# Splitting a weight row in one operation of 1024 columns instead of two of 512

## The chip, the cores and the metric

The kernel runs on one core of one Trainium2 chip. The metric is the device time of one execution in microseconds. Before the change the median of three runs is 2045.59 us (2045.24 to 2045.6).

## What is computed

A decoder trunk of two layers over 256 tokens with a model width of 2048, all in fp32. Cut to what matters here:

```python
# layer 0
u = rms_norm(x) @ w_in[0]
pooled = causal_multiscale_pool(u[..., :1536])            # 4 groups, windows 2/4/8/16
token_out = einsum(pooled, pool_w) * pool_scale
mem_out = memory_cross_attention(u[..., 1536:], mem, w_mem_kv[0])
x = x + concat([token_out, mem_out]) @ w_out[0]
x = x + squared_relu(rms_norm(x) @ w_ff1[0]) @ w_ff2[0]   # 2048 -> 8192 -> 2048
# shared keys and values, then layer 1
k1, k2, v = split(rms_norm(x) @ w_kv)
u = rms_norm(x) @ w_in[1]
token_out = rms_norm(differential_attention(q1, q2, k1, k2, v))
mem_out = memory_cross_attention(u[..., 1536:], mem, w_mem_kv[1])
x = x + concat([token_out, mem_out]) @ w_out[1]
x = x + squared_relu(rms_norm(x) @ w_ff1[1]) @ w_ff2[1]
```

## The kernel before

**Weights as rows and quads.** All weights lie in HBM in the order of use, in rows of 128 partitions by 1024 columns. A row holds eight blocks of 128 columns, or two **quads** of four blocks (512 columns). SP loads a row with one DMA (L139) into one of four `raw` buffers (RAWS, L27), up to three rows ahead of the row that is being prepared (LOADS).

**The split.** TensorE multiplies in fp32r, a rounded fp32, and the kernel keeps precision by splitting each weight in two: `Feed._split` (L152) lets ScalarE (ACT) copy the weight into `hi_ring` rounded (L157), and VectorE (DVE) subtract that from the weight and put the remainder into `lo_ring` (L158). Both rings have six slots of 512 columns (SLOTS); `Feed._slots` (L143) gives out one slot or two adjacent ones, goes back to slot 0 where two don't fit, and says no while one of them is in use. The activations are split in the same way (L369, L300).

**The order of the work.** The program runs twice. The first run, on a stand-in, only lists what is needed: every quad is a job `("N", number)` in `Plan.jobs`. `Plan.close` (L70) makes of it `prep`, the order in which the weights are split, and `loads`, the order of the rows. In the second run `Feed.quad` (L208) calls `Feed.fill` (L196) as each quad begins, and `fill` prepares everything up to three jobs ahead (AHEAD) through `Feed._prepare` (L162). `Feed.used` (L226) gives a quad's slot back when its four blocks have been multiplied. Small work of other parts (scores, transposes, sums) is queued with `at` and issued by `tick` after each quad, between the matmuls. The engines' instruction orders are settled when the kernel is compiled, by the dependences between the tiles.

**Who reads a quad.** `a_part` (L377) takes two blocks at a time: two matmuls of the rounded parts with 512 columns of split activations (L391), then two of the remainders with 256 (L393). `wide_step` (L412) reads a whole quad as the moving side, for two halves of the tokens, three matmuls each: rounded, rounded, remainder (L417, L418, L419). `c_tile` (L400) takes one block with three matmuls of 256 columns (L405 to L407), and `group_w` (L1013) does the same for the pooling maps.

**Stages in time.** From the start: memory keys and values of layer 0 (`wide_step`, 32 quads, with the loads and splits of the memory and of x beside them), memory queries, the pooling mixer (`u`, `pw`) with the memory attention between, the output projection (`out_tiles`, L1028, `wo`), the feed-forward block (`ffn`, L648). Then the shared keys and values, memory keys and values of layer 1, the queries with the differential attention between them, memory queries, output projection, feed-forward block.

`out_tiles` begins with three output tiles side by side, one in each of three PSUM banks, from those inputs that are there first; when the last inputs are there, the three are finished one after the other and the fourth tile takes the bank of the first, once `resid_add` (L637) has added both its halves to the residual (L638, L639). GpSimd (POOL) squares and sums the residual beside it (L624, L625) for the next norm, which PE reads as `st_x` (L430).

**The feed-forward block** multiplies half of its second weight by a scheme of seven products for eight. For these its rows go to `slab` buffers, and jobs `("S", slab, part)` split them, some with 1024 columns at once, in the same rings. Three of its output tiles carry one slab's jobs, so a slab job is never more than a few quads away there. Jobs `K` and `L` are sums that DVE makes for a slab.

Of the kernel before, what the change touches and what calls it, by code (L numbers as in the profile page):

```python
# [55 lines left out]
class Plan:  # L56
# [13 lines left out]
    def close(self):  # L70
        prep = []
        for job in self.jobs:

            late = job[0] == "S" and job[1] % 32 > 28
            if job[0] == "S" and job[2] == 0 and not late:
                prep.insert(max(0, len(prep) - KOFF), ("K", job[1]))
            if late and job[2] == 1:
                prep.append(("L", job[1]))
            prep.append(job)
        self.prep = prep  # L80
        self.where = {job: i for i, job in enumerate(prep)}
        self.loads = []
        self.need = {}
        for p in prep:
            if p[0] == "K":
                self.loads += [("S", p[1], 0), ("S", p[1], 1)]
            elif p[0] == "L":
                self.loads.append(("S", p[1], 1))
            elif p[0] == "S" and p[2] == 0 and ("S", p[1], 0) not in self.loads:
                self.loads.append(("S", p[1], 0))  # L90
            elif p[0] == "N" and p[1] % 2 == 0:
                self.loads.append(("N", p[1] // 2))
            self.need[p] = len(self.loads) - 1
        rows = sorted(self.loads, key=lambda r: r[0] == "N" and 8 * r[1] + 8 > self.npos)
        self.row = {r: h for h, r in enumerate(rows)}
        of = {}
        pos = 0
        for what in self.entries:
            of.setdefault(pos // 8, []).append(what)
            pos += what[4]  # L100
        self.order = []
        for r in rows:
            self.order += of[r[1]] if r[0] == "N" else self.slabs[r[1]][r[2]]


class Feed:
# [55 lines left out]
    def _prepare(self, p):  # L162
        sub, add = self.nc.vector.tensor_sub, self.nc.vector.tensor_add
        self.load(self.plan.need[p] + 1 + LOADS)
        if p[0] == "N":
            r = ("N", p[1] // 2)
            c = p[1] % 2 * 512
            if not self._split(p, self.raw[r][:, c : c + 512], 1):
                return False
            if c:  # L170
                del self.raw[r]
            return True
        ra, rb = self.raw[("S", p[1], 0)], self.raw.get(("S", p[1], 1))
        t1 = self.t1[1 if p[1] % 32 > 28 else p[1] % 2]

        def both():
            t2 = rb[:, 0:512].unsqueeze(1).to_broadcast([P, 2, 512])
            two = ra.rearrange("p (a c) -> p a c", a=2)
            sub(two, t2, two)

        if p[0] in "KL":
            add(t1, ra[:, 0:512], rb[:, 0:512])
            sub(rb[:, 0:512], t1, rb[:, 512:1024])
            if p[0] == "L":
                both()
            return True
        src, n = ((ra, 2), (t1, 1), (rb, 2), (ra, 2))[p[2]]
        if not self._split(p, src, n):
            return False
        if p[2] == 0 and ("K", p[1]) in self.plan.need:  # L190
            both()
        if p[2] == 3:
            del self.raw[("S", p[1], 0)], self.raw[("S", p[1], 1)]
        return True
# [1182 lines left out]
```

## Time and profile before

| | |
|---|---|
| median of 3 runs | 2045.59 us |
| the profiled execution | 2044.93 us |
| its span, first to last instruction | 2043.1 us |
| PE busy, matmuls | 2037.2 us, 11060 |
| DVE busy | 1716.2 us, 3215 instructions |
| ACT busy | 1349.8 us, 2505 instructions |
| POOL busy | 51.9 us, 67 instructions |
| DMA | 390.75 MB, 191 GB/s on average |
| casts of `raw` on ACT (L157) | 1193 of 512 columns, 620 ns each |
| remainders of `raw` on DVE (L158) | 1193 of 512 columns, 695 ns each |
| granted TensorE clock | 1.0 of full speed |

PE is TensorE's matmuls, and their ends are modelled, so a busy PE may still hide short waits. In the lists of groups a line has the source line, the engine, the operation, the tile that is written and the tiles that are read, the shape and the count; behind the first bar the busy time in us and the mean of one in ns, behind the second the idle time of the engine just before, and what ended most of it. In the timeline a line begins with the start in us from the span's begin and the length in us, and ends with the idle time before it in square brackets, if there was any. A remainder's span on DVE or a cast's on ACT overlaps that of the next operation a little, so that operations queued without a gap start closer together than their lengths.

### The profile page before, as it was taken

To read this page: it belongs to the slowest core of one execution; us is meant where nothing else is said; L and a number is where in the kernel's file an instruction comes from. 1 tells how busy PE (TensorE), PEld (TensorE's weight loads), DVE (VectorE), ACT (ScalarE), POOL (GpSimd) and SP (SyncE) were. 2 spreads that over 40 slices of the span, in tenths; PEclk is the share of its full clock that TensorE was granted. 3 is DMA by queue.
4 is the path that set the end of the run, shared out by engine and by line. 5 is a ranking of instruction groups with operands and counts; after the bars stand their busy time and mean duration, and the time that the engine had idled before them with its cause. 6 is when DMAs were issued, how large, how long until landed. Compare 5 with 4: busy or idle time off the path is not lost.

```text
span 2043.1 us, 32257 instructions
## 1 busy us (share of the span) xinstructions
PE 2037.2 (100%) x11060; PEld 1755.3 (86%) x11060; DVE 1716.2 (84%) x3215; ACT 1349.8 (66%) x2505; POOL 51.9 (3%) x67
## 2 busy tenths in 40 slices
PE   9999999999999999999999999999999999999999
PEld 8888888888888888888888888888888888888888
DVE  8888889889879978999766687889879978988997
ACT  7765566666666756768665697566657666666764
POOL 0001200000000000000000000310000000000000
PEclk9999999999999999999999999999999999999999
DMA  9556556555555555655565543656555555565564
GB/s 314 178 181 190 188 174 206 197 196 197 186 201 202 189 207 191 207 169 182 194 228 186 170 140 103 196 166 207 196 196 205 186 196 196 186 210 195 196 209 135
DMA packets 110470, 390.75 MB, mean 191 GB/s; under 512 B 12256, under 2 KB 14944, under 8 KB 110304
## 3 DMA queue, kind: packets, MB, share of 16 engines
q1 hardware_dynamic: 110160, 388.59, 57.1%
q8 instruction: 86, 1.41, 0.3%
q14 instruction: 80, 0.66, 0.1%
q10 hardware_dynamic: 144, 0.10, 0.0%
HBM read 386.54 MB, written 2.10 MB: 190 GB/s over the span
## 4 chain that ended last, share of the span: by engine, by line
PE 99%; ACT 1%; DVE 1%; issue 0%
PE x_bank L391 33%; PE x_bank L393 16%; PE wo L391 6%; PE p L746 5%; PE p L747 5%; PE p L748 5%; PE wo L393 3%; PE u L391 2%; PE ff L391 2%; PE u L393 1%; PE k L417 1%; PE k L419 1%; PE v L417 1%; PE k L418 1%; PE v L419 1%; PE v L418 1%
## 5 line engine op out<-in xcount | busy, mean ns | idle before, releaser
L157 ACT CAST hi_ring<-raw 128x512 fp32r<-128x512 f32 x1193 | 736.7, 620 | 529.5 <-PE x_bank L391 308.0
L158 DVE TENSOR_TENSOR lo_ring<-raw,hi_ring 128x512 fp32r<-128x512 f32 x1193 | 817.2, 695 | 206.7 <-ACT hi_ring L157 165.5
L391 PE MATMUL x_bank<-fx,hi_ring 128*128 128x512 f32 x1920 | 602.1, 395 | 0.0
L393 PEld LDWEIGHTS x_bank<-fx,lo_ring 128*128 128x128 f32 x1920 | 361.0, 188 | 83.6
L393 PE MATMUL x_bank<-fx,lo_ring 128*128 128x256 f32 x1920 | 377.4, 278 | 0.0
L391 PEld LDWEIGHTS x_bank<-fx,hi_ring 128*128 128x128 f32 x1920 | 301.4, 189 | 9.3
L391 PE MATMUL x_bank<-z,hi_ring 128*128 128x512 f32 x960 | 301.1, 395 | 0.0
L158 DVE TENSOR_TENSOR lo_ring<-slab,hi_ring 128x1024 fp32r<-128x1024 f32 x188 | 230.1, 1224 | 54.3 <-ACT hi_ring L157 53.6
L157 ACT CAST hi_ring<-slab 128x1024 fp32r<-128x1024 f32 x188 | 196.9, 1047 | 73.1 <-PE x_bank L391 36.2
L393 PEld LDWEIGHTS x_bank<-z,lo_ring 128*128 128x128 f32 x960 | 180.5, 188 | 41.7
L393 PE MATMUL x_bank<-z,lo_ring 128*128 128x256 f32 x960 | 188.8, 278 | 0.0
L391 PE MATMUL wo<-cat,hi_ring 128*128 128x512 f32 x512 | 162.5, 398 | 0.5 <-DVE resid L639 0.5
L391 PEld LDWEIGHTS x_bank<-z,hi_ring 128*128 128x128 f32 x960 | 151.9, 189 | 6.5 <-ACT room L672 0.4
L393 PEld LDWEIGHTS wo<-cat,lo_ring 128*128 128x128 f32 x512 | 95.9, 188 | 21.7
L672 ACT COPY room<-x_bank 128x512 f32<-128x512 f32 x180 | 104.9, 583 | 2.0 <-PE x_bank L393 2.0
L393 PE MATMUL wo<-cat,lo_ring 128*128 128x256 f32 x512 | 101.4, 279 | 0.0
L746 PE MATMUL p<-hi_ring,sit 128*128 128x512 f32 x256 | 100.5, 393 | 0.0
L747 PE MATMUL p<-hi_ring,sit 128*128 128x512 f32 x256 | 100.2, 391 | 0.0
L748 PE MATMUL p<-lo_ring,sit 128*128 128x512 f32 x256 | 99.7, 389 | 0.0
L391 PEld LDWEIGHTS wo<-cat,hi_ring 128*128 128x128 f32 x512 | 79.1, 189 | 2.2 <-PE wo L393 0.9
L717 ACT ACTIVATE room<-room 128x256 f32<-128x256 f32 x128 | 53.2, 416 | 39.1 <-DVE room L300 39.1
L746 PE MATMUL p<-hi_ring,z 128*128 128x512 f32 x192 | 75.2, 392 | 0.0
(313 smaller groups left out, 3102.3 us busy)
## 6 DMA issues: line engine op xcount, KB each, us to landing
raw<-in_w SPq DMA_DIRECT2D x595, 512.0 KB, 4.0
slab<-in_w SPq DMA_DIRECT2D x124, 512.0 KB, 3.3
resid<-in_x SPq DMA_DIRECT2D x8, 256.0 KB, 5.9
room<-in_w SPq DMA_DIRECT2D x4, 512.0 KB, 4.2
memraw<-in_mem SPq DMA_DIRECT2D x4, 512.0 KB, 3.6
out_y<-resid SPq DMA_DIRECT2D x16, 128.0 KB, 1.8
memraw<-in_mem SPq DMA_DIRECT2D x7, 256.0 KB, 6.3
raw<-in_w SPq DMA_DIRECT2D x3, 256.0 KB, 3.5
```

Of the source, the lines that this page charges most:

```text
L157: self.nc.scalar.copy(hi, src)
L158: self.nc.vector.tensor_sub(lo, src, hi.bitcast(F32))
L391: nc.tensor.matmul(ps, hi, xs[:, k, :], start=first and c == 0, stop=False)
L393: nc.tensor.matmul(ps[:, T : 2 * T], lo, xs[:, k, 0:T], start=False, stop=last and c == len(ks) - 1,)
L417: nc.tensor.matmul(ps[t], xl, hi, start=k == 0, stop=False)
L418: nc.tensor.matmul(ps[t], xh, hi, start=False, stop=False)
L419: nc.tensor.matmul(ps[t], xh, lo, start=False, stop=k == NK - 1)
L672: nc.scalar.copy(x, ps)
L717: at(3, lambda: nc.scalar.activation(stage[i % 8], y[:, 0:T], AF.Square))
L746: nc.tensor.matmul(ps, a[1], hi, start=first, stop=False)
L747: nc.tensor.matmul(ps, a[0], hi, start=False, stop=False)
L748: nc.tensor.matmul(ps, a[0], lo, start=False, stop=last)
```

## The change

`Plan.close` makes a set `wide` of the rows whose two quads are split in one operation. A row is in it if it isn't one of the first two, if it is whole, and if no job other than a quad's stands within eight places of its first quad in the order of preparation. That leaves out nearly all of the feed-forward blocks, whose slab jobs are always near. `_prepare` then splits a wide row with its first quad: one cast and one subtraction of 1024 columns, into two adjacent slots. The two halves are handed to the two quads, each with its own slot to give back, and the second quad's preparation has nothing left to do.

```diff
@@ -91,6 +91,14 @@
             elif p[0] == "N" and p[1] % 2 == 0:
                 self.loads.append(("N", p[1] // 2))
             self.need[p] = len(self.loads) - 1
+
+        other = [i for i, p in enumerate(prep) if p[0] != "N"]
+        self.wide = {
+            p[1] // 2
+            for i, p in enumerate(prep)
+            if p[0] == "N" and p[1] % 2 == 0 and p[1] >= 4 and 4 * p[1] + 8 <= self.npos
+            and all(abs(i - o) > 8 for o in other)
+        }
@@ -165,6 +173,16 @@
         if p[0] == "N":
             r = ("N", p[1] // 2)
             c = p[1] % 2 * 512
+            if r[1] in self.plan.wide:
+                if c:
+                    return True
+                if not self._split(p, self.raw[r], 2):
+                    return False
+                hi, lo, (a, b) = self.split[p]
+                self.split[p] = hi[:, 0:512], lo[:, 0:512], (a,)
+                self.split[("N", p[1] + 1)] = hi[:, 512:1024], lo[:, 512:1024], (b,)
+                del self.raw[r]
+                return True
             if not self._split(p, self.raw[r][:, c : c + 512], 1):
                 return False
```

## The prediction

> **What bounds the kernel now.** I read the page's first part, then the chain of work that ended last, then the groups of the two lines that split weights (L157, the rounded copy on ACT; L158, the remainder on DVE).
>
> ```profile
> span 2043.1 us, 32257 instructions
> ## 1 busy us (share of the span) xinstructions
> PE 2037.2 (100%) x11060; PEld 1755.3 (86%) x11060; DVE 1716.2 (84%) x3215; ACT 1349.8 (66%) x2505; POOL 51.9 (3%) x67
> ...
> PE 99%; ACT 1%; DVE 1%; issue 0%
> ...
> L157 ACT CAST hi_ring<-raw 128x512 fp32r<-128x512 f32 x1193 | 736.7, 620 | 529.5 <-PE x_bank L391 308.0
> L158 DVE TENSOR_TENSOR lo_ring<-raw,hi_ring 128x512 fp32r<-128x512 f32 x1193 | 817.2, 695 | 206.7 <-ACT hi_ring L157 165.5
> ...
> L158 DVE TENSOR_TENSOR lo_ring<-slab,hi_ring 128x1024 fp32r<-128x1024 f32 x188 | 230.1, 1224 | 54.3 <-ACT hi_ring L157 53.6
> L157 ACT CAST hi_ring<-slab 128x1024 fp32r<-128x1024 f32 x188 | 196.9, 1047 | 73.1 <-PE x_bank L391 36.2
> ```
>
> PE is on the chain 99% of the time and is idle for 5.9 us of 2043.1. A busy PE could still hide waits, so I took the steps from one matmul's start to the next in the timeline: 512 columns take 227 to 236 ns and 256 columns 112 to 120 ns almost everywhere, a quad (four 128-column blocks) 1.39 us in the narrow products and 1.36 us in the wide steps, in every stage alike. So PE runs at its own pace. ACT idles 529.5 us before its splits, mostly until PE gives a ring slot back: the splits run ahead as far as the ring lets them.
>
> **What the change removes and adds.** From the plan's order of jobs, rows 2 to 87, 275 to 407 and 595 are wide: 220 rows, so 440 of the 1193 narrow splits of each engine become 220 of 1024 columns. The slab rows above show that operation already: 1047 ns on ACT, 1224 ns on DVE. Queued without a gap, narrow splits start 526 ns apart on ACT and 603 on DVE, slab splits 955 and 1142. A row saves 2 x 526 - 955 = 97 ns on ACT and 2 x 603 - 1142 = 64 ns on DVE: 21 us and 14 us in all. They lie beside PE's matmuls, so I count them as **0**; if ACT or DVE set the pace of those stretches they would be a gain of at most this size, but PE there is busy 665.4 of 667 us (windows 10 to 265, 945 to 1357).
>
> **Slack.** What counts is whether a quad's parts are ready before PE reads them. Now a slot comes free when the quad six before is done, 5 quads (6.97 us) before its next use. Taking every split's end against the start of the first matmul that reads it, the median slack in the stretches to be changed is 6.3 us (rounded part) and 5.9 us (remainder). Afterwards a row needs both slots of the row three before, so it starts 4 quads (5.57 us) before its first use: 5.57 - 1.05 = 4.5 us, and 4.5 - 1.22 = 3.3 us for the remainder. Where the remainder is later than usual today (1.8 us of slack at 1216 us, 2.0 at 1284, 2.2 at 146, at least 2.7 elsewhere after 25 us), DVE's queue sets it, and the first half comes only 1224 - 691 = 0.53 us later: 1.3 us stay. So no split becomes late in the steady part: **0**. The bound is the 1.0 us by which a backlog as long as the longest of today (5.9 - 1.8 = 4.1 us) would exceed 3.3 us. The ring's one odd start, at row 275 (slots 1-2, 3-4, then 0-1), leaves only three quads, but transposes stretch these to 5.1 us by today's starts (940.4 to 945.5): 0.
>
> **The start** is the exception: row 2 is the first wide one and has almost no slack. Here are ACT, DVE and PE around it in the timeline (start, length, engine, line, what it writes and reads, and how often):
>
> ```profile
> 10.73 2.29 ACT L157 CAST hi_ring<-raw 128x512 fp32r<-128x512 f32 x4
> ```
> ```profile
> 11.61 2.49 DVE L158 TENSOR_TENSOR lo_ring<-raw,hi_ring 128x512 fp32r<-128x512 f32 x4
> ```
> ```profile
> 12.14 0.39 PE L417 MATMUL mk<-hi_ring,mems 128*128 128x512 f32 x1
> 12.37 0.39 PE L418 MATMUL mk<-hi_ring,mems 128*128 128x512 f32 x1
> 12.60 0.39 PE L419 MATMUL mk<-lo_ring,mems 128*128 128x512 f32 x1
> ```
>
> The four splits are quads 4 to 7. Quad 4's remainder ends at 11.61 + 0.69 = 12.30, 0.30 us ahead of L419 at 12.60. Wide, the cast runs 10.73 to 11.78, the remainder from about 11.81 to 13.03: L419 starts 0.43 us late, about 0.45 with the hand-over. Row 3 then ends near 14.2, for a need at 15.3; row 4 near 17.4, for 18.0. PE never gets this back: **+0.45 us** (0 if the engines' order puts this split earlier, 1.2 if its cast also slips by one activation and row 4 is late as well).
>
> **The waits PE has today** in the stretches touched are short, and they are what could go or grow. Two stand where the first three output tiles close together and the fourth wants the first one's bank, with one in the attention:
>
> ```profile
> 179.88 0.62 ACT L157 CAST hi_ring<-raw 128x512 fp32r<-128x512 f32 x1 [0.61 <-PE wo L391]
> ...
> 180.54 0.69 DVE L158 TENSOR_TENSOR lo_ring<-raw,hi_ring 128x512 fp32r<-128x512 f32 x1
> ...
> 181.15 0.42 DVE L639 TENSOR_TENSOR resid<-resid,wo 128x256 f32<-128x256 f32 x1
> ...
> 181.71 0.70 PE L391 MATMUL wo<-cat,hi_ring 128*128 128x512 f32 x2 [0.21 <-DVE resid L639]
> ```
> ```profile
> 1261.95 0.81 PE L592 MATMUL mt<-const,att 128*128 128x128 f32 x4 [0.76 <-DVE att L586]
> ```
> ```profile
> 1277.29 0.70 PE L391 MATMUL wo<-cat,hi_ring 128*128 128x512 f32 x2 [0.33 <-DVE resid L639]
> ```
>
> Beyond the usual step from start to start these three cost PE 0.37, 0.92 and 0.49 us, and the eight next ones 0.19 to 0.31 each: 3.56 us in all, at transposes and scores whose inputs come late from ACT or DVE, and at banks. A split stands in front of the awaited operation in each of the three. A wide one is 0.43 us (ACT) or 0.53 us (DVE) longer if it still stands there, and takes 0.62 or 0.69 us away if that place is a row's second half. Half of each is a gain of about 0.1 us per wait, less than the scatter: **0**, bounds -3.56 (all gone) and +4.7 (the second rival).
>
> **DMA and queues.** Loads stay one per row. A raw buffer comes free when the row's remainder is taken, and SP's next load waits for that; the page gives 4.0 us to landing where a row lasts 2.79 us and four buffers turn, some 8 us of cover. POOL's squares (L624, L625) share the output stages with DVE. At 183.63 a narrow remainder took 1.23 us beside POOL's sum (183.50 to 184.30), and 30 of them together took 7.3 us more than usual, so half as many operations meet this half as often; PE waited for none of them.
>
> Against the change speaks a rule of the Trainium skill, "SBUF — State Buffer", section "SBUF: two separate sides": a DVE operation with two SBUF inputs and a GpSimd operation that reads SBUF exclude each other for the whole instruction. The long rows agree with it. By it a wide remainder would shut POOL out for 0.53 us longer; POOL's last sum ends at 256.71 + 1.07 = 257.78 and PE reads it at 259.82, so even two such delays would end 1.0 us early and the sum would be the same as by the rows.
>
> **Sum.** The profiled execution took 2044.93 us, 1.83 us around its span of 2043.1. 2044.93 + 0.45 = 2045.4; it lies 0.66 us under the median of the three runs (2045.59), so on that median I say **2046.0 us**.
>
> **Rivals.**
> 1. *Attention and banks gain.* ACT and DVE are fullest from 1140 to 1280 us (111.4 and 114.3 of 140), and each row gives them time back. If all 3.56 us went: 2045.59 + 0.45 - 3.56 = 2042.5, still within 0.2% (4.1 us). For it: every one of those waits comes from ACT or DVE. Against: a longer operation is also a longer one to stand behind. 0.13.
> 2. *Slower: a wide remainder in front of the bank's release.* DVE works in order; at 180.12 it had added one half of the first tile, then took a remainder whose cast had waited for a ring slot, and only then L639. Wide, the cast may wait one quad more (1.39 us) and both are longer (0.43 + 0.53): 2.35 us per place, two places 4.7 us, with the start 2045.59 + 5.15 = 2050.7. It decides once 3.65 us of it fall due, so when both places are hit nearly in full; one place alone gives 2048.4, within 0.2%. For it: the very order stands in the lines above. Against: the first three tiles end 1.05 us apart and there the adds may come first. 0.08.
> 3. *The engines' order shifts.* ACT's first cast (4.70) runs before the first activation (5.23), which the program issues first, so the order on an engine is made from expected times, and 440 shorter operations can turn it elsewhere, also in the feed-forward parts. A few waits of the largest size seen in the chain (0.9 us) give +2; slower by 0.2% needs five. 0.05, of which 0.03 beyond 0.2%.
> 4. *Faster by over 0.2%.* More than every wait of the stretches touched would have to go. 0.02.
> 5. *It does nothing*, the rows not becoming wide: 2045.6. 0.02.
>
> **Chances.** The forecast itself has 0.70, with a range of its own of 2044.3 to 2047.6. Faster by over 0.2% (about what a measurement of this kernel can tell from no change): 0.02; slower: 0.08 + 0.03 = 0.11; within: 0.87. The range reaches down to 2043.1, which keeps most of the first rival, and up to 2049.7, which takes in one bank place in full and half of the second.
>
> **What would show it.** 220 casts and remainders `<-raw` of 1024 columns near 1.05 and 1.22 us, 753 narrow ones left; DVE's busy time down by 14 (the queued saving) to 440 x 695 - 220 x 1224 = 37 us, and ACT's by 21 to 440 x 620 - 220 x 1047 = 42 us; PE's busy time unchanged within 1 us; L419 of the third row at 13.0 to 13.1 instead of 12.60; the waits at 181, 1262 and 1277 us each between gone and 2.9 us. The prediction is wrong if a new wait for `hi_ring` or `lo_ring` shows on PE after 20 us, if PE's steps get shorter in the changed stretches, or if the feed-forward stretches change length.

## The result, and the profile after

The changed kernel takes **2048.84 us** in the median of 21 runs (2048.29 to 2050.42), against 2045.59 us for the kernel before in as many (2045.21 to 2046.68): 3.25 us more, a ratio of 1.0016 (interval 1.001 to 1.0022). That is slower by more than the scatter and within 0.2%. The profiled execution took 2048.7 us with a span of 2046.9 us, 3.8 us longer than that of before. Three executions in the runs further down, one of `rows2_15` and two of the kernel before, took 2365 to 6175 us: the medians there contain them and would move by less than 0.1 us without them, and the ratios leave them out.

The page of the kernel after begins so; behind it are its groups by form for the two splitting lines, which have moved to L165 (ACT) and L166 (DVE). Other lines behind the class `Feed` have moved by 18: L391 is now L409, L393 is L411, L638 and L639 are L656 and L657.

```profile
span 2046.9 us, 31467 instructions
...
PE 2039.9 (100%) x11060; PEld 1754.6 (86%) x11060; DVE 1691.1 (83%) x2995; ACT 1313.5 (64%) x2285; POOL 71.9 (4%) x67
```
```profile
L166 DVE TENSOR_TENSOR lo_ring<-raw,hi_ring 128x512 fp32r<-128x512 f32 x753 | 510.4, 687 | 93.2 <-ACT hi_ring L165 63.3 <-PE p L765 26.9
L165 ACT CAST hi_ring<-raw 128x512 fp32r<-128x512 f32 x753 | 466.2, 620 | 325.0 <-PE x_bank L409 305.6 <-PE ff L409 8.6 <-DMA raw<-in_w 3.9
L166 DVE TENSOR_TENSOR lo_ring<-raw,hi_ring 128x1024 fp32r<-128x1024 f32 x220 | 270.7, 1232 | 139.4 <-ACT hi_ring L165 138.4
L165 ACT CAST hi_ring<-raw 128x1024 fp32r<-128x1024 f32 x220 | 231.3, 1052 | 224.2 <-PE wo L409 51.0 <-issue 41.7 <-PE v L436 27.0
```

The chain of work that ended last gives PE 49% where before it gave 99%, but only because it is followed back no further than the key rows' transpose at 1024.99 us; from there to the end it is PE's in both.

The change does on ACT and DVE what it says: 220 wide splits of 1052 and 1232 ns, 753 narrow ones left, 25 us less work on DVE and 36 us less on ACT. PE does the same 11060 matmuls and takes longer from the first to the last. Of the 3.8 us of its span only 1.1 us are more idle time (7.0 instead of 5.9 us); 2.7 us are more busy time: a late input can show as a longer step of a matmul instead of a gap, as at 13.16 us, where PE takes 0.44 us to the next matmul instead of 0.23 and isn't idle. The view of what PE waited for shows where one should look (engine, line and tile, what released it, us in all, times, the longest):

```profile
PE wo L409 <- DVE resid L657: 0.7, 2, 0.5
PE wo L409 <- DVE cat L318: 0.6, 1, 0.6
PE dt L1244 <- DVE att L318: 0.3, 1, 0.3
PE wo L411 <- DVE lo_ring L166: 0.2, 1, 0.2
...
PE mt L610 <- DVE att L604: 0.2, 1, 0.2
PE tr L553 <- DVE krow L534: 0.2, 1, 0.2
```

Before, this list held the wait at the start (`warm`, 1.0 us; 1.1 us now), `mt` with 0.8 and `resid` with 0.5 us. The wait of `mt` has shrunk to 0.2 and that of `resid` has grown to 0.7; `cat`, `dt`, `lo_ring` and `tr` are new. They are short, and they leave out the longer steps, so I set the start of the same matmul in both traces against each other at points where PE's order is the same. The difference grows (us, after minus before):

| stage (us from the span's start, before) | grows by |
|---|---|
| to 11.3, no wide row yet | 0.56 |
| 11 to 60: the rest of the memory keys and values | 0.39 |
| 60 to 159: memory queries and the pooling mixer | -0.15 |
| 159 to 190: three output tiles side by side, layer 0 | **0.95** |
| 190 to 935: rest of the output projection, feed-forward | -0.10 |
| 935 to 1005: end of feed-forward, keys | 0.24 |
| 1005 to 1030: values, transposes of the key rows | **0.37** |
| 1030 to 1149: memory keys and values, first queries | -0.01 |
| 1149 to 1258: queries with attention between them | **0.72** |
| 1258 to 1290: three output tiles side by side, layer 1 | **0.83** |
| 1290 to the end | 0.01 |

The first row is scatter. At 11.3 us the traces of the other kernels of this study stand 0.1 to 1.6 us behind that of the kernel before, and those with the same code up to there take up nearly all of that range (0.14 to 1.53 us). ACT's casts of the first rows wait for their loads there, 2.7 us in the trace before and 3.9 us in the one after. From 11.3 us on the difference is 3.24 us, and the four bold stages hold 2.87 of them. These are short stages in which small work hangs between the matmuls. In the steady stretches, nothing of note is lost or gained.

### The profile page after: what moved, and what is told of

It reads as the page before. It is cut to its first block, busy times and chain, and to the rows that moved or that the text cites. A ratio compares the mean times of both kernels' runs of the same rounds, so it can differ in the third digit from the quotient of the medians.

```text
span 2046.9 us, 31467 instructions
## 1 busy us (share of the span) xinstructions
PE 2039.9 (100%) x11060; PEld 1754.6 (86%) x11060; DVE 1691.1 (83%) x2995; ACT 1313.5 (64%) x2285; POOL 71.9 (4%) x67
## 4 chain that ended last, share of the span: by engine, by line
PE 49%; ACT 1%; DVE 0%; issue 0%
PE x_bank L409 16%; PE x_bank L411 8%; PE wo L409 3%; PE p L764 3%; PE p L765 2%; PE p L766 2%; PE wo L411 1%; PE q L437 1%; PE q L435 1%; PE q L436 1%; PE ff L409 1%; PE v L435 1%; PE v L436 1%; PE v L437 1%; PE ff L411 0%; PE mq L424 0%
## 5 line engine op out<-in xcount | busy, mean ns | idle before, releaser
L165 ACT CAST hi_ring<-raw 128x512 fp32r<-128x512 f32 (+1 forms) x973 | 697.5, 718 | 549.3 <-PE x_bank L409 305.6
L166 DVE TENSOR_TENSOR lo_ring<-raw,hi_ring 128x512 fp32r<-128x512 f32 (+1 forms) x973 | 781.0, 810 | 232.6 <-ACT hi_ring L165 201.7
L409 PE MATMUL x_bank<-fx,hi_ring 128*128 128x512 f32 x1920 | 601.8, 395 | 0.0
L411 PEld LDWEIGHTS x_bank<-fx,lo_ring 128*128 128x128 f32 x1920 | 360.6, 188 | 84.0
L411 PE MATMUL x_bank<-fx,lo_ring 128*128 128x256 f32 x1920 | 377.2, 278 | 0.0
L409 PEld LDWEIGHTS x_bank<-fx,hi_ring 128*128 128x128 f32 x1920 | 301.3, 189 | 9.4
L409 PE MATMUL x_bank<-z,hi_ring 128*128 128x512 f32 x960 | 300.9, 395 | 0.0
L166 DVE TENSOR_TENSOR lo_ring<-slab,hi_ring 128x1024 fp32r<-128x1024 f32 x188 | 230.0, 1223 | 54.9 <-ACT hi_ring L165 54.1
L165 ACT CAST hi_ring<-slab 128x1024 fp32r<-128x1024 f32 x188 | 196.8, 1047 | 73.5 <-PE x_bank L409 36.4
L411 PEld LDWEIGHTS x_bank<-z,lo_ring 128*128 128x128 f32 x960 | 180.3, 188 | 41.9
L411 PE MATMUL x_bank<-z,lo_ring 128*128 128x256 f32 x960 | 188.6, 278 | 0.0
L409 PE MATMUL wo<-cat,hi_ring 128*128 128x512 f32 x512 | 163.6, 399 | 1.4 <-DVE resid L657 0.7
L409 PEld LDWEIGHTS x_bank<-z,hi_ring 128*128 128x128 f32 x960 | 151.8, 189 | 6.5 <-ACT room L690 0.4
L411 PEld LDWEIGHTS wo<-cat,lo_ring 128*128 128x128 f32 x512 | 96.1, 188 | 22.3 <-DVE lo_ring L166 0.6
L411 PE MATMUL wo<-cat,lo_ring 128*128 128x256 f32 x512 | 102.2, 279 | 0.2 <-DVE lo_ring L166 0.2
L409 PEld LDWEIGHTS wo<-cat,hi_ring 128*128 128x128 f32 x512 | 79.1, 189 | 3.8 <-DVE cat L318 1.9
```

The costliest lines, as they stand in the source:

```text
L165: self.nc.scalar.copy(hi, src)
L166: self.nc.vector.tensor_sub(lo, src, hi.bitcast(F32))
L409: nc.tensor.matmul(ps, hi, xs[:, k, :], start=first and c == 0, stop=False)
L411: nc.tensor.matmul(ps[:, T : 2 * T], lo, xs[:, k, 0:T], start=False, stop=last and c == len(ks) - 1,)
```

## The experiments

My theory after this comparison: the lost time comes from the *length* of one operation. ACT and DVE take their operations one after the other in the compiled order, so what PE needs next may stand behind a split of 1.05 or 1.23 us that PE needs only much later. Against it stood three rivals: preparing both quads at one point of the order and taking two ring slots at once makes splits late, whatever the operations' length (my slack step was wrong); ACT's longer cast does it and DVE's remainder doesn't; or one or two rows do it all, and leaving them narrow gives the time back. The intervals of the ratios are about 0.0009 to each side (1.8 us), so a difference of medians of a few tenths proves nothing. The growth by stage is finer: where a kernel's code is unchanged between 11.3 us and the end, it comes out between -0.08 and +0.11 us, except from 60 to 159 us, where 0.19, and from 935 to 1005 us, where 0.24 us came without any change.

### One stage at a time

The set of wide rows is cut to those of one or two stages. Together the four kernels have all wide rows but the last one (595).

```diff
+        self.wide &= set(range(2, 16))                          # rows2_15
+        self.wide &= set(range(44, 88))                         # rows44_87
+        self.wide &= set(range(341, 408))                       # rows341_407
+        self.wide &= set(range(16, 44)) | set(range(275, 341))  # rows16_43_275_340
```

> Only rows 2 to 15 are wide (the first stage, memory keys and values of layer 0). Theory of single waits (the loss is a handful of places where a wide split stands in front of what PE needs next): quad 4's remainder is late by 0.3 to 0.45 us and nothing else, so +0.4 us (2045.9 to 2046.1). Rival, the changed order of instructions (the loss comes from the order as a whole and does not split up by stage): some other size, and the four parts of this call do not add up to the 3.25 us of the whole. Second rival, the start itself (0.6 us at the very first matmul belongs to the change): +1.0 us.

> Only rows 44 to 87 are wide (end of the pooling mixer, output projection of layer 0, first feed-forward tiles). Single waits: PE waits about 0.8 to 0.9 us for the last pooled inputs at the second output tile, because a wide split stands ahead of their splits on ACT and DVE, and as long as before for the first bank: +0.9 to +1.1 us (2046.5 to 2046.7). Order as a whole: another size.

> Only rows 341 to 407 are wide (queries, differential attention, memory queries, output projection of layer 1). Single waits: the largest part, +1.3 to +1.7 us (2046.9 to 2047.3), spread over transposes of the attention. If instead ACT and DVE were short of time there and the saved time counted, it would be faster than before, by up to 1 us.

> Only the quiet stages are wide: rows 16 to 43 (memory queries and most of the pooling mixer) and 275 to 340 (shared keys and values, memory keys and values of layer 1). Single waits: +0.4 to +0.7 us (2046.0 to 2046.3), from the key rows' transposes near 1024 us. If the slack of 3.3 us is what the steady stages need, there is no PE wait for hi_ring or lo_ring here. If the shorter lead of the ring costs something everywhere, it must show here: over +1 us.

| wide rows | median us | to before | ratio (interval) | grows in its own stages |
|---|---|---|---|---|
| 2 to 15 | 2045.96 | +0.29 | 1.0002 (0.9993 to 1.0011) | 0.41 (11 to 60) |
| 44 to 87 | 2046.29 | +0.62 | 1.0003 (0.9994 to 1.0012) | 0.95 (159 to 190) |
| 341 to 407 | 2046.92 | +1.25 | 1.0006 (0.9997 to 1.0015) | 0.69 (1149 to 1258), 0.81 (1258 to 1290) |
| 16 to 43, 275 to 340 | 2045.77 | +0.10 | 1.0001 (0.9992 to 1.001) | 0.37 (1005 to 1030), -0.24 (60 to 159) |

Each stage's loss comes with its own rows, and with the same size as in the whole change (0.39, 0.95, 0.72, 0.83, 0.37). In the traces the four sums from 11.3 us on (0.23, 1.22, 1.61, 0.37) make 3.43 us beside the 3.24 of the whole. The medians add up only to 2.26 of 3.25 us; that 1 us lies within the intervals, and I can't assign it. Three of the four expectations named more than the medians show (+0.9 to +1.1, +1.3 to +1.7 and +0.4 to +0.7 us in the last three rows of the table).

Now the places. At 179 us in the kernel after, ACT and DVE split row 59 just as the pooling mixer ends (start, length, engine, line, what it writes and reads; the idle time before it in brackets):

```profile
177.99 1.05 ACT L165 CAST hi_ring<-raw 128x1024 fp32r<-128x1024 f32 x1 [0.49 <-PE pw L1039]
...
178.94 0.83 ACT L387 ACTIVATE cat<-pw,param 128x256 fp32r<-128x256 f32 x2
...
179.07 1.23 DVE L166 TENSOR_TENSOR lo_ring<-raw,hi_ring 128x1024 fp32r<-128x1024 f32 x1 [1.05 <-ACT hi_ring L165]
...
180.21 0.87 DVE L318 SCALAR_TENSOR_TENSOR cat<-pw,param,cat 128x256 fp32r<-128x256 f32 x2
...
180.75 0.73 PE L409 MATMUL wo<-cat,hi_ring 128*128 128x512 f32 x2 [0.65 <-DVE cat L318]
```

PE waits for `cat` (the last pooled products, split for the output projection), and L318, which makes it, stands behind the wide remainder. The wide cast has its part too: DVE idles 1.05 us until it is done, and ACT's own piece of `cat` (L387) stands behind it. PE had no such wait before. But the weight loads ahead of its matmuls (PEld) did, at the same place in the kernel before:

```profile
177.74 0.69 DVE L158 TENSOR_TENSOR lo_ring<-raw,hi_ring 128x512 fp32r<-128x512 f32 x1 [0.35 <-ACT hi_ring L157]
...
178.35 0.93 DVE L300 SCALAR_TENSOR_TENSOR cat<-pw,param,cat 128x256 fp32r<-128x256 f32 x2
...
178.88 0.30 PEld L391 LDWEIGHTS wo<-cat,hi_ring 128*128 128x128 f32 x2 [0.25 <-DVE cat L300]
```

A remainder stood in front of `cat` there too, and `cat` came just in time: a weight load waited 0.25 us and PE did not.

The key rows at 1024 us show the same with a short operation. L534 (0.28 us, the last piece of a rotated key row) stands behind a wide remainder, and PE's transposes wait for it; in the kernel before, where it is L516, a remainder of 0.69 us stands there and PE doesn't wait. After, then before:

```profile
1023.51 1.22 DVE L166 TENSOR_TENSOR lo_ring<-raw,hi_ring 128x1024 fp32r<-128x1024 f32 x1
...
1024.65 0.28 DVE L534 TENSOR_TENSOR krow<-ra,rb 128x128 f32<-128x128 f32 x1
...
1024.99 0.55 PE L553 MATMUL tr<-const,krow 128*128 128x128 f32 x3 [0.15 <-DVE krow L534]
```
```profile
1021.16 0.29 DVE L516 TENSOR_TENSOR krow<-ra,rb 128x128 f32<-128x128 f32 x1
...
1022.68 0.49 PE L535 MATMUL tr<-const,krow 128*128 128x128 f32 x3
```

This place did have slack: before, the piece was done at 1021.45, 1.2 us ahead of the transposes. The transposes begin 1.89 us later on the clock than before (1024.57 for the first one), L534 3.49 us later. So it is 1.6 us late, which one wide remainder (0.53 us longer than a narrow one) doesn't account for. A second one, at 1019.39 us, stands in front of the same chain of small operations, with one operation of 0.48 us (`mems`) more ahead of it than before, and the delays add up.

In the attention from 1149 to 1258 us the long operation in front is ACT's. PE's first wait for `dt` (transposes of the attention weights) is at 1163.07 us; ACT's part of their making (L1229, L1211 before), which DVE's L318 needs, stands behind a cast. After, then before:

```profile
1158.53 1.05 ACT L165 CAST hi_ring<-raw 128x1024 fp32r<-128x1024 f32 x1 [2.12 <-PE q L436]
...
1159.61 0.56 ACT L1229 ACTIVATE att<-s,mx,qy 128x256 f32<-128x256 f32 x1
...
1163.07 0.52 PE L1244 MATMUL dt<-const,att 128*128 128x128 f32 x3 [0.26 <-DVE att L318]
```
```profile
1156.28 0.62 ACT L157 CAST hi_ring<-raw 128x512 fp32r<-128x512 f32 x1 [1.83 <-PE q L418]
1157.00 0.56 ACT L1211 ACTIVATE att<-s,mx,qy 128x256 f32<-128x256 f32 x1
...
1160.47 0.52 PE L1226 MATMUL dt<-const,att 128*128 128x128 f32 x3
```

On the clock L1229 starts 2.61 us later than L1211 did, where PE's matmuls at 1155.87 us (before 1153.62) are only 2.25 us later; before, PE didn't wait.

The place at 1264 us is of another kind, and it is a late split:

```profile
1261.14 1.05 ACT L165 CAST hi_ring<-raw 128x1024 fp32r<-128x1024 f32 x1 [0.15 <-PE wo L409]
...
1263.50 1.22 DVE L166 TENSOR_TENSOR lo_ring<-raw,hi_ring 128x1024 fp32r<-128x1024 f32 x1
...
1264.77 0.50 PE L411 MATMUL wo<-cat,lo_ring 128*128 128x256 f32 x2 [0.24 <-DVE lo_ring L166]
```

This is row 376. The compiled order of PE's instructions shows why it is late: where three output tiles go side by side, PE multiplies two blocks (the ninth and tenth) of the first tile and of the second ahead of the whole part of the third tile that the program issues first. So PE reads row 376's first quad about 8 us ahead of its turn, in the kernel before as well, where its remainder was done 3.78 us early (1257.00 for 1260.79). Wide, the split must wait for both slots of row 373, the cast begins at 1261.14, DVE has other work until 1263.50, and the remainder ends only 0.06 us before the matmul that has waited 0.24 us for it.

### Pairing, or the length on one engine

These three kernels prepare the same 220 rows, both quads at one point, with two adjacent slots, as the change does. They differ from it only in the length of the operations.

```diff
-                if not self._split(p, self.raw[r], 2):
+                a = self._slots(2)
...
+                for s in (slice(0, 512), slice(512, 1024)):   # wide_act: slice(0, 1024) alone
+                    nc.scalar.copy(hi[:, s], src[:, s])
+                for s in (slice(0, 512), slice(512, 1024)):   # wide_dve: slice(0, 1024) alone
+                    nc.vector.tensor_sub(lo[:, s], src[:, s], hi[:, s].bitcast(F32))
```

> All 220 rows are prepared as in the changed kernel (both quads at the first quad's place, into two adjacent slots), but with two casts and two remainders of 512 columns. Theory that the length of the single operation costs (1.05 and 1.22 us that nothing can pass): under 1 us of the 3.25 are left, +0.3 to +1.0 us. Rival, the pairing itself (the second half is taken a quad earlier, and waits a quad longer for its slot, in front of other work): +2.5 to +3.5 us.

> All 220 rows paired; the cast is one operation of 1024 columns on ACT, the remainder two of 512 on DVE. If DVE's long remainder is what PE waits behind (the key rows at 1024 us, the pooled splits and the banks after it): +1.0 to +2.0 us, and no wait at the key rows' transpose. If ACT's long cast is: +2.5 us or more.

> All 220 rows paired; the cast is two operations of 512 columns on ACT, the remainder one of 1024 on DVE, which waits for both casts. If DVE's long remainder is what PE waits behind: +2.0 to +3.2 us. If ACT's long cast is: +0.5 to +1.5 us.

| cast, remainder | median us | to before | ratio (interval) | 159-190 | 1005-1030 | 1149-1258 | 1258-1290 |
|---|---|---|---|---|---|---|---|
| narrow, narrow (`pairs`) | 2045.50 | -0.16 | 1.0 (0.9991 to 1.0009) | 0.00 | 0.00 | -0.02 | -0.02 |
| wide, narrow (`wide_act`) | 2045.93 | +0.27 | 1.0002 (0.9993 to 1.0011) | 0.37 | 0.01 | 0.43 | -0.92 |
| narrow, wide (`wide_dve`) | 2048.12 | +2.46 | 1.0012 (1.0003 to 1.002) | 1.43 | 0.85 | 0.42 | -0.41 |
| wide, wide (the change) | 2048.84 | +3.25 | 1.0016 (1.001 to 1.0022) | 0.95 | 0.37 | 0.72 | 0.83 |

Pairing costs nothing, less than I had expected, so the first rival falls: with narrow operations the same lead and the same slots give 0.00 to -0.02 us in all four stages. That the operations' length costs the time is thereby shown; whether only by the waiting behind a longer operation, or also by the order that the compiler makes of other lengths, is not. With DVE's remainder alone wide the kernel is 2.46 us slower, and 1 lies outside the interval of its ratio, so the second rival, in which the remainder costs nothing, falls as well.

How much of the 3.25 us is the cast's and how much the remainder's is not shown. For the +0.27 of `wide_act` the interval includes 1, I had expected more in either case, and by stage it is made of losses (0.37 and 0.43 in the table, 0.56 from 60 to 159 us) and a gain of 0.92. `wide_dve` loses more than the change from 159 to 190 and from 1005 to 1030 us. From 1149 to 1290 us the change loses 1.55 us, while `wide_dve` loses 0.01 and `wide_act` gains 0.49. Single waits can be put down to an engine: for `cat` in layer 0 PE waits 0.15 us with the long cast alone, 0.28 with the long remainder alone, 0.65 with both. The two waits for `dt` in the attention (0.26 and 0.24 us) come with the long cast (0.25 and 0.28 in `wide_act`); in `wide_dve` the trace shows no wait of PE from 1149 to 1258 us.

`wide_dve` also shows in full the very mechanism that the prediction's second rival had named for the first bank:

```profile
181.92 1.23 DVE L187 TENSOR_TENSOR lo_ring<-raw,hi_ring 128x1024 fp32r<-128x1024 f32 x1
...
183.06 0.41 DVE L663 TENSOR_TENSOR resid<-resid,wo 128x256 f32<-128x256 f32 x1
...
183.63 0.70 PE L415 MATMUL wo<-cat,hi_ring 128*128 128x512 f32 x2 [0.97 <-DVE resid L663]
```

The wide remainder stands between the two adds of the first tile (the first one at 181.51), and the fourth tile waits 0.97 us for its bank, against 0.21 before. In the change itself, at that place, DVE's adds come ahead of the remainder, and the wait stays as it was, 0.23 us at 183.47.

### Taking out single rows

If single rows at the places shown do the harm, narrow splits for them alone give it back. Row 59 is the one at 179 us; `minus5` keeps the whole change and takes out row 59, row 305 (key rows), and rows 376, 378 and 379 (third and fourth output tile).

```diff
+        self.wide &= set(range(44, 88)) - {59}      # no59
+        self.wide -= {59, 305, 376, 378, 379}       # minus5
```

> Rows 44 to 87 are wide as in the run of that stage, except row 59, whose cast (ACT at 178 us) and remainder (DVE at 179 us) stand in front of the splits of the last pooled outputs. Single waits: PE's wait at the second output tile goes, and the profile's loss between 160 and 190 us falls from 0.95 to under 0.3 us; the time is at most 0.2 us over the kernel before (2045.6 to 2045.9). If the stage loses its time by the changed order as a whole or by the ring's shorter lead, one row of 44 changes nothing: +0.6 us as with all of them.

> The whole change without five of its 220 rows: 59 (pooled outputs, 179 us), 305 (key rows, 1024 us), 376, 378 and 379 (mixed attention and first bank, 1263 to 1277 us). Single waits: the loss of 3.25 us falls by 0.95 + 0.4 + 0.8, to +1.0 us, give or take 0.5 (2046.1 to 2047.2). Order as a whole, or a cost per wide row: five rows of 220 change under 0.3 us (2048.6 or more).

`no59`: 2045.09 us, 0.57 less than before, ratio 0.9998 (0.9989 to 1.0007), where 2045.6 to 2045.9 was expected. With row 59 wide the stage from 159 to 190 us grows by 0.95; without it, it shrinks by 0.36. One narrow row is worth 1.31 us there. DVE's order at the place:

```profile
178.52 0.69 DVE L167 TENSOR_TENSOR lo_ring<-raw,hi_ring 128x512 fp32r<-128x512 f32 x1 [0.31 <-ACT hi_ring L166]
...
179.13 0.93 DVE L319 SCALAR_TENSOR_TENSOR cat<-pw,param,cat 128x256 fp32r<-128x256 f32 x2
...
179.22 1.41 PE L410 MATMUL wo<-cat,hi_ring 128*128 128x512 f32 x5
```

`cat` is in time, and the next wide remainder (182.02) comes after the adds of the first tile, so the wait for the bank is gone too.

`minus5`: 2049.57 us, 4.05 more than before, ratio 1.0021 (1.0011 to 1.0031), where my theory of single rows expected most of the loss back. From 159 to 190 us it did come back (-0.36 instead of +0.95), and the wait for `lo_ring` at 1264 us is gone. But 1005 to 1030 us grew by 1.00 instead of 0.37 (PE now waits 0.59 us for ACT's copy of a key transpose, `tr` at 1028.49), and 1258 to 1290 us by 1.45 instead of 0.83 (one wait of 0.9 us for `cat`, and `mt` again with 0.7). The start of that trace is late by chance (1.55 us at 11.3 us); from there on it loses 3.0 us, about as much as the whole change. So the third rival falls too: the rows aren't independent culprits. Where I looked, the compiled order of the instructions had come out differently with the edit, and another operation stood behind a long one.

### A kernel from the best parts

From the runs so far I took what had gained: rows 16 to 24 (60 to 159 us had shrunk), 44 to 87 without 59, and for rows 374 to 407 a wide cast with narrow remainders, since `wide_act` had shrunk by 0.92 from 1258 to 1290 us. `rows16_24` and `act374` are two of these parts by themselves.

```diff
+        self.wide &= set(range(16, 25))     # rows16_24
+        self.wide &= set(range(374, 408))   # act374: one cast of 1024, two remainders of 512
+        self.wide &= set(range(16, 25)) | (set(range(44, 88)) - {59}) | set(range(374, 408))   # best: fully wide below row 300, as act374 above it
```

> Only rows 16 to 24 wide (memory queries). In the runs with that stage wide the profile gains 0.6 to 0.7 us between 60 and 76 us and loses 0.5 later. If the gain belongs to these rows: -0.5 to -0.7 us (2045.0). If it hangs on the order of the whole stage: within 0.2 us of before.

> Only rows 374 to 407 paired, with one cast of 1024 columns and two remainders of 512. The run with that form in all rows gained 0.9 us between 1258 and 1290 us. If it belongs to these rows (ACT gets time, DVE is held no longer): -0.6 to -0.9 us (2044.8 to 2045.1). If it made up for delays that the earlier rows caused: 0 to +0.2 us.

> Rows 16 to 24 and 44 to 87 without 59 wide, rows 374 to 407 with one cast and two remainders. If single waits add up: -0.6 (first rows) - 0.5 (as measured for rows 44 to 87 without 59) - 0.8 = -1.9 us (2043.8), faster than both kernels. If the parts disturb each other: between -0.5 and 0 us.

| kernel | median us | to before | ratio (interval) | 60-159 | 159-190 | 1258-1290 |
|---|---|---|---|---|---|---|
| `rows16_24` | 2045.62 | +0.10 | 1.0 (0.9991 to 1.0009) | -0.23 | 0.00 | 0.00 |
| `act374` | 2046.68 | +1.16 | 1.0005 (0.9996 to 1.0014) | 0.19 | -0.02 | **1.20** |
| `best` | 2046.38 | +0.86 | 1.0004 (0.9995 to 1.0013) | -0.25 | -0.36 | **1.15** |

Rows 16 to 24 alone change the time by nothing that could be told from scatter, where I had expected -0.5 to -0.7 us. The combination failed at the part that I had counted as its gain. Rows 374 to 407 are split in the same form in `wide_act` and in `act374`, and from 1258 to 1290 us one shrinks by 0.92 and the other grows by 1.20 us, outside both of its expectations. First `act374`, then `wide_act`, at the normalisation of the memory attention (L615 and L610, one line of the program) that PE's transposes wait for:

```profile
1261.49 1.29 DVE L192 TENSOR_TENSOR lo_ring<-raw,hi_ring 128x512 fp32r<-128x512 f32 x2 [0.50 <-ACT hi_ring L190]
...
1262.90 0.62 DVE L615 TENSOR_SCALAR att<-att,mm_rec 128x256 f32<-128x256 f32 x2
...
1263.31 0.81 PE L621 MATMUL mt<-const,att 128*128 128x128 f32 x4 [0.56 <-DVE att L615]
```
```profile
1261.44 0.62 DVE L610 TENSOR_SCALAR att<-att,mm_rec 128x256 f32<-128x256 f32 x2
...
1261.92 0.27 PE L616 MATMUL mt<-const,att 128*128 128x128 f32 x1
...
1262.18 0.69 DVE L187 TENSOR_TENSOR lo_ring<-raw,hi_ring 128x512 fp32r<-128x512 f32 x1
```

In the first, two queued remainders come before the normalisation; in the second, they come after it, and PE doesn't wait. Both were settled when the kernel was compiled: the compiled order of PE differs between them as well (in `wide_act` the remainder products of the second tile's ninth and tenth block stand behind the third tile's first part, in `act374` ahead of it). Why the order falls one way or the other stays open; no run here controlled it. The quickest kernel of the study is `no59`, and its interval doesn't exclude that it is as quick as the kernel before.

## Why the prediction was right or wrong

The kernel is slower by less than 0.2%, as said, and inside the stated range. That is owed in good part to luck: 0.4 us was said and 3.25 measured, the time lies above the 2044.3 to 2047.6 that I gave the forecast itself, and only the room left for the second rival, at another place, takes it in.

**The saved time, 0: right.** DVE is busy 25.1 us less and ACT 36.3 us less, inside the 14 to 37 and 21 to 42 said, and no stretch got quicker for it by more than scatter.

**No split late in the steady part, 0: right but for one place.** The median slack of a row's first quad after is 4.5 us (rounded) and 3.7 us (remainder), where 4.5 and 3.3 were worked out (the bound given there, 1.0 us, should have been 4.1 - 3.3 = 0.8); PE's steps in the steady stretches are unchanged; the odd ring start left 0.67 us at its tightest (row 277), and PE didn't wait. The failure is row 376: 0.24 us of PE's idle time at 1264.77, a sign that the prediction itself had named as proof against it. The step matched splits and matmuls by the order in which the program issues them, and in the three side-by-side tiles PE doesn't keep that order.

**The start, +0.45: right.** The compiled order of the split is as worked out, and PE takes up the third row's remainder as soon as it is there:

```profile
12.32 2.56 DVE L166 TENSOR_TENSOR lo_ring<-raw,hi_ring 128x1024 fp32r<-128x1024 f32 x2
...
13.60 0.50 PE L437 MATMUL mk<-lo_ring,mems 128*128 128x512 f32 x1
```

L437 (L419 before) starts 1.00 us later than the 12.60 of before. The delay before the first wide row is 0.56 us of it; the stage from 11 to 60 us grew by 0.39 in this kernel and by 0.41 with rows 2 to 15 alone. Had I compared only the one start, I would have doubled the step.

**The waits PE has today, 0: this step failed.** It weighed waits that were already there and set gains against losses. Of its three, `mt` at 1262 us did gain (0.8 to 0.2 us), the bank at 1277 lost 0.13, and the bank at 181.7 kept its wait (0.21 to 0.23). What the step left out is work with *no* wait before: `cat` (0.65 us), the key rows (0.15), the attention's transposes (0.26 and 0.24). The first of these had no slack, and the kernel before showed it, in the weight loads' idle time and not in PE's; the key rows had 1.2 us, and the delays of several operations ahead of them used it up. So the term of 0 measured 2.9 us (the four bold stages, with row 376's late split in the last), inside its bounds of -3.56 and +4.7. One of the signs named for the forecast failed with it: PE's busy time, which was to stay within 1 us, grew by 2.7.

A rule of the Trainium skill bears on this step, and I had not weighed it ("Perfetto Trace Analysis", section "Optimizing Scalar/DVE Operations"): grouping operations raises an engine's throughput if the engine is saturated; if it isn't and makes gaps on other engines, breaking its instructions up may let work end sooner. These runs agree with the second half: DVE is 83% busy in `wide_dve`, and the same rows with remainders in halves (`pairs`) are 2.62 us quicker. No run here has a saturated DVE, so the first half isn't tested.

**The second rival** had the right mechanism and the wrong place. A wide split in front of what PE needs next is what costs the time, at the places shown, and its sole place was to be the bank; that is shown by `wide_dve` (0.97 us), not by the change. **The third rival** was worth more than its 0.05: the order of the engines shifts with edits, as `minus5` and `act374` show, though nothing shifted in the feed-forward parts (190 to 935 us: -0.10; from 1290 on: 0.01). **The first rival**, a gain in attention and banks, is refuted for the whole change (+0.72 and +0.83), and true of `wide_act` in one stage by the luck of an order.

**POOL: the harm was right at 0, the direction wrong.** I expected half as many meetings with DVE. PE waited for none, but POOL became busier with the same 67 instructions, 51.9 to 71.9 us; nearly all of it is in the two output projections. The length of the remainders isn't enough to explain that, for in `wide_dve` they are as long and POOL is busy for 47.5 us. Which of the two starts first differs. POOL's sum and DVE's remainder at the same point of the output projection, in the change and then in `wide_dve`:

```profile
202.75 1.83 POOL L643 TENSOR_TENSOR acc<-acc,psq 128x256 f32<-128x256 f32 x1
```
```profile
202.75 1.23 DVE L166 TENSOR_TENSOR lo_ring<-raw,hi_ring 128x1024 fp32r<-128x1024 f32 x1 [0.77 <-ACT hi_ring L165]
```
```profile
202.48 0.89 POOL L649 TENSOR_TENSOR acc<-acc,psq 128x256 f32<-128x256 f32 x1
```
```profile
202.80 1.65 DVE L187 TENSOR_TENSOR lo_ring<-raw,hi_ring 128x1024 fp32r<-128x1024 f32 x1
```

Where both start together, POOL's sum takes 1.83 us and the remainder its usual 1.23; where the sum is ahead by 0.32 us, it takes 0.89 and the remainder 1.65. The sums of the next three output tiles repeat this (1.82 to 1.83 against 0.88 to 0.89 us). The rule weighed in the prediction (the Trainium skill, "SBUF — State Buffer", section "SBUF: two separate sides": the two engines exclude each other for a whole instruction) agrees with this.

## What to carry to other kernels

Joining two operations into one saves busy time on an engine that works in order and makes whatever stands behind it wait longer; here, where neither engine was the bound, only the second counted. So before joining, look for the places where short work feeds the bottleneck through the same engine, and work out their slack: a place with no wait on PE can have none at all (look at the weight loads' waits too), and the delays of several operations in one chain can use up a microsecond of it. And where the instructions' order is settled by a compiler, a gain of a few tenths at one place isn't a part that can be carried into another version: it has to be measured there again.

## What the runs showed of the hardware

- DVE and POOL lengthen each other, and it depends on which starts first: at the same point of two kernels POOL's sum took 1.83 us (started with a remainder of 1.23) or 0.89 (started 0.32 us ahead of a remainder that then took 1.65). Over the kernel POOL's 67 instructions took 71.9 or 47.5 us with equally long remainders on DVE. PE waited for none of it.
- Joining 220 pairs of operations on DVE alone cost 2.46 us and on ACT alone 0.27 us (within the scatter), although both run beside PE and neither was full (83% and 64% busy). By stage the two don't add up to the change with both.
- The first 11.3 us of the profiled executions differ by up to 1.5 us with the same code there, more than most effects in this study; differences of single spans mean little without the comparison by stage.
